# A two-layer hybrid block on one core: two small tiles take other places in SBUF

## The chip, the core and the metric

The kernel runs on one core of one Trainium2 chip. The metric is the time on the device in microseconds (us). Three timed runs of the kernel before gave 1068.19, 1068.74 and 1072.17 us; the median is 1068.74. A time is told below as ns where it belongs to one instruction.

## The reference, cut to what matters

Two layers work on a sequence of 256 tokens with 1024 features, in float32. Each layer is a mixer and a feed-forward part, both with a residual:

```
for l in range(2):
    h = rms_norm(x, norm_mix_w[l])
    q,k,v,qi,ki,wi,z,xbc,dt,g_attn,g_ssd = split(h @ w_in[l])
    a = attention over the 64 best keys by an index score      # 8 heads
    b = chunked state-space scan of silu(conv(xbc)), gated by silu(z), group norm
    x = x + (sigmoid(g_attn) * (a @ w_proj_attn) + sigmoid(g_ssd) * (b @ w_proj_ssd)) @ w_out
    h = rms_norm(x, norm_ffn_w[l])
    u = conv(h @ w_up) ; x = x + (silu(gate(u)) * val(u)) @ w_down
out = rms_norm(x, norm_final_w)
```

Nothing of this is touched by the change. By far the most work is the projections: 320 weight chunks of 128 rows are loaded, each is split into a high and a low part, and each is multiplied in three passes (high weights with the high and with the low part of the activations, low weights with the high part).

## The kernel before, in words

**How a projection runs.** Weights come by DMA from the SP queue into five `raw` buffers (L174). ScalarE casts a chunk to its high part `whi` (L199), VectorE subtracts to get `wlo` (L200). `n_outer` and `k_outer` then issue matmuls of 128 weight columns with 256 moving columns: `feed_high` (L376 with the high part of the activations, L377 with the low part), then `feed_low` (L382). In these the activations are the moving operand and the weights are loaded ahead. In the first projections of a layer (L548, L551, L554, function `wide`) it is the other way round: the weights move, in 308 or 512 columns, and the activations are loaded.

**Which tile holds what.** All activations and some weights lie in a pool `act`, where a tile is placed once by its tag, one after the other in the order of first use, and later tiles with the same tag take the same place. The tags that matter:

- `Bm`, `Cm`, `lg0`, `lg1`: the normed input of a layer or of the feed-forward part as `uh` (high) and `ul` (low), later the scan's B and C and the attention's logits.
- `big0`, `big1`: token-major projections, then `bc` (the scan's decay factors, read by the matmuls of L731), then `bL`, the low part of the scan's output. They also hold two early weight chunks (`ebig`).
- `s0` to `s3`: queries and keys, then `bH` (the high part of the scan's output), then `fH0`, `fL0`, `fH1`, `fL1` (the first third of the feed-forward's hidden values), and early weight chunks `es`.
- `hxh`, `hxl`: the scaled normed input (`hxh`, `hxl`) and the merged mixer output (`mH`, `mL`). `z0` to `z3` and `x0` to `x3` hold `aH`, `aL`, the scan's values, and `fH2` to `fH5` with their low parts.
- `wd` (320 bytes in a partition) holds the step sizes and index weights, `dec` (128 bytes) the decays of the scan's first chunk.

The weight buffers `whi`, `wlo` lie in a pool of their own ahead of `act`; all six start 64 bytes past a multiple of 256.

**What sets the order.** The engines' streams are written out by a scheduler at build time; helper work of attention and scan is laid between the projections as lanes of generators. A layer runs: input projections (to about 60 us in the first layer), convolution tiles with attention and scan between them (60 to 206), gates with z and the group norms (206 to 280), the scan's projection from `bH` and `bL` (280 to 325), the output projection from `mH`, `mL` (325 to 347), the feed-forward's first chunks from `uh`, `ul` (347 to 373), its other chunks from `hxh`, `hxl` (373 to 471), and the way down from `fH`, `fL` (471 to 531). The second layer repeats that about 525 us later. On the way down the first four output tiles run with the hidden values as the outer loop; the other four take, each in turn, 24 matmuls from `fH0`, `fL0`, `fH1`, `fL1`, then 24 from the next two pairs, then 18 from the last two. Each layer's group norms and norms put a matmul of `dg` with `ones` (L298, twice each) between the others.

Of the kernel before, what the change touches and what calls it, by code (L numbers as in the profile page):

```python
# [9 lines left out]
F32 = mybir.dt.float32  # L10
# [8 lines left out]
P = 128  # L19
# [44 lines left out]
def hybrid_kernel(ctx: ExitStack, tc: tile.TileContext, a: dict, out: bass.AP):  # L64
# [5 lines left out]
    act = ctx.enter_context(tc.tile_pool(name="act", bufs=1))  # L70
# [72 lines left out]
    def side(lane, gen, delay):  # L143


        lanes[lane].append([st["now"] + delay, gen])
# [100 lines left out]
    def sm(name, l=None, n=None):  # L247
        o, w = _SMALL[name]
        v = small[:, o:o + w]
        if l is not None:  # L250
            v = v[:, l * (w // L):(l + 1) * (w // L)]
        return v
# [150 lines left out]
        return ps  # L403


    nrm = Normed(sm("nmw", 0))
    side("norm", nrm.factor(), KD + 1)

    for l in range(L):

        tok = [act.tile([P, 8 * T], F32, name=f"big{t}", tag=f"big{t}")[:, :1856] for t in range(2)]
        V = [act.tile([P, T], F32, name=f"V{t}", tag=f"V{t}") for t in range(2)]
        wd = act.tile([P, 2, 40], F32, name="wd", tag="wd")

        def rotate(v, t, heads, dim, rot, o):
            h = rot // 2
# [83 lines left out]
        dA = act.tile([P, 2, 32], F32, name="dA", tag="dA")  # L500
        Pc = act.tile([P, 2, 32], F32, name="Pc", tag="Pc")
        nP = act.tile([P, 2, 32], F32, name="nP", tag="nP")
        dec = act.tile([P, 32], F32, name="dec", tag="dec")

        prd = dram.tile([32, 2, P], F32, name=f"prd{l}")

# [513 lines left out]
```

## Time and profile before

| what | value |
|---|---|
| median of the timed runs | 1068.74 us |
| time of the profiled execution | 1067.94 us |
| its span | 1066.1 us |
| mean granted TensorE clock, as a share | 0.999 |
| TensorE busy | 1056.1 us, 99% |
| VectorE busy | 860.7 us, 81% |
| ScalarE busy | 694.8 us, 65% |
| GpSimd busy | 81.4 us, 8% |
| mean DMA rate | 180 GB/s |

TensorE has work all the time, so the time is the sum of the paces at which its matmuls follow each other. A matmul's own duration in the profile (some 280 ns) spans several that are in flight, and is no measure of the pace; the pace is the distance between the starts of two neighbours, which the timeline shows, or a stretch divided by the matmuls that start in it.

### The profile page before, as it was taken

To read this page: it belongs to the slowest core of one execution; us is meant where nothing else is said; L and a number is where in the kernel's file an instruction comes from. 1 tells how busy PE (TensorE), PEld (TensorE's weight loads), DVE (VectorE), ACT (ScalarE), POOL (GpSimd) and SP (SyncE) were. 2 spreads that over 40 slices of the span, in tenths; PEclk is the share of its full clock that TensorE was granted. 3 is DMA by queue.
4 is the path that set the end of the run, shared out by engine and by line. 5 is a ranking of instruction groups with operands and counts; after the bars stand their busy time and mean duration, and the time that the engine had idled before them with its cause. 6 is when DMAs were issued, how large, how long until landed. Compare 5 with 4: busy or idle time off the path is not lost.

```text
span 1066.1 us, 22377 instructions
## 1 busy us (share of the span) xinstructions
PE 1056.1 (99%) x8713; PEld 1020.8 (96%) x8713; DVE 860.7 (81%) x1652; ACT 694.8 (65%) x1285; POOL 81.4 (8%) x88
## 2 busy tenths in 40 slices
PE   9999999999999999999999999999999999999997
PEld 8799999999999999999997999899999999999997
DVE  6999979789677898886577999887895878988643
ACT  6769878567555566665465789775674556666552
POOL 3000000033001000000100000000420020000011
PEclk9999999999999999999999999999999999999999
DMA  8655445555677256667645654554666761666661
GB/s 309 208 185 191 141 140 179 148 181 176 201 235 247 80 159 197 195 194 240 195 134 167 220 159 139 168 168 146 179 183 207 259 218 42 195 197 195 185 184 51
DMA packets 53688, 191.81 MB, mean 180 GB/s; under 512 B 6176, under 2 KB 7216, under 8 KB 52560
## 3 DMA queue, kind: packets, MB, share of 16 engines
q1 hardware_dynamic: 51840, 180.71, 54.5%
q0 software_dynamic: 1600, 9.69, 2.4%
q8 instruction: 68, 1.11, 0.4%
q14 instruction: 36, 0.29, 0.1%
q10 hardware_dynamic: 144, 0.01, 0.0%
HBM read 189.26 MB, written 1.11 MB: 179 GB/s over the span
## 4 chain that ended last, share of the span: by engine, by line
PE 87%; DMA 6%; DVE 3%; issue 1%; ACT 1%; POOL 0%; SPq 0%; POOLq 0%; DVEq 0%; ACTq 0%
PE acc L376 22%; PE acc L377 22%; PE acc L382 22%; DMA raw<-in_wu_dram 5%; PE acc L548 3%; PE acc L551 3%; PE acc L554 3%; PE sa L377 2%; PE sa L376 2%; PE sa L382 2%; PE sb L731 2%; DVE ul L330 1%; PE sa L615 1%; PE sa L640 1%; DVE wlo L200 1%
## 5 line engine op out<-in xcount | busy, mean ns | idle before, releaser
L199 ACT CAST whi<-raw 128x1024 fp32r<-128x1024 f32 (+2 forms) x320 | 332.0, 1040 | 225.2 <-PE acc L377 137.0
L200 DVE TENSOR_TENSOR wlo<-raw,whi 128x1024 fp32r<-128x1024 f32 (+2 forms) x320 | 386.5, 1210 | 102.1 <-ACT whi L199 95.4
L376 PE MATMUL acc<-hxh,whi 128*128 128x256 f32 x1456 | 352.3, 282 | 0.0
L377 PE MATMUL acc<-hxl,whi 128*128 128x256 f32 x1456 | 349.7, 280 | 0.0
L377 PEld LDWEIGHTS acc<-hxl,whi 128*128 128x128 f32 x1456 | 274.3, 188 | 1.8 <-issue 1.6
L376 PEld LDWEIGHTS acc<-hxh,whi 128*128 128x128 f32 x1456 | 274.3, 188 | 1.5 <-issue 1.2
L382 PE MATMUL acc<-hxh,wlo 128*128 128x256 f32 x1456 | 200.6, 279 | 0.0
L382 PEld LDWEIGHTS acc<-hxh,wlo 128*128 128x128 f32 x1456 | 182.0, 188 | 0.6 <-issue 0.5
L675 DVE SCALAR_TENSOR_TENSOR cv<-acc,half,cv 128x255 f32<-128x255 f32 (+2 forms) x144 | 66.6, 472 | 4.1 <-ACT cv L673 3.7
L877 DVE SCALAR_TENSOR_TENSOR cv<-acc,small,cv 128x255 f32<-128x255 f32 (+1 forms) x144 | 68.5, 477 | 1.3
L343 POOL TENSOR_TENSOR ssq<-ssq,sq 128x256 f32<-128x256 f32 x30 | 27.8, 928 | 498.4 <-ACT sq L339 495.1
L376 PE MATMUL acc<-fH,whi 128*128 128x256 f32 x264 | 64.0, 277 | 0.0
L377 PE MATMUL acc<-fL,whi 128*128 128x256 f32 x264 | 63.9, 277 | 0.0
L377 PEld LDWEIGHTS acc<-fL,whi 128*128 128x128 f32 x264 | 49.6, 188 | 0.0
L376 PEld LDWEIGHTS acc<-fH,whi 128*128 128x128 f32 x264 | 49.5, 188 | 0.0
L377 PE MATMUL acc<-bL,whi 128*128 128x256 f32 x192 | 47.6, 282 | 0.0
L376 PE MATMUL acc<-bH,whi 128*128 128x256 f32 x192 | 47.5, 279 | 0.0
L721 ACT ACTIVATE bc<-bc,nP 128x128 f32<-128x128 f32 x128 | 40.5, 392 | 7.5 <-DMA bc<-prd 7.4
L830 POOL TENSOR_TENSOR ssq<-ssq,sq 128x256 f32<-128x256 f32 x24 | 32.2, 1343 | 136.5 <-ACT sq L829 136.1
L875 ACT ACTIVATE cv<-acc,small 128x256 f32<-128x256 f32 x72 | 40.6, 563 | 0.1
L382 PE MATMUL acc<-fH,wlo 128*128 128x256 f32 x264 | 37.8, 277 | 0.0
L377 PEld LDWEIGHTS acc<-bL,whi 128*128 128x128 f32 x192 | 36.2, 188 | 0.0
(346 smaller groups left out, 2011.4 us busy)
## 6 DMA issues: line engine op xcount, KB each, us to landing
raw<-in_wu_dram SPq DMA_DIRECT2D x88, 512.0 KB, 4.0
raw<-in_wx_dram SPq DMA_DIRECT2D x48, 512.0 KB, 3.7
raw<-in_wd_dram SPq DMA_DIRECT2D x38, 512.0 KB, 3.7
raw<-in_wz_dram SPq DMA_DIRECT2D x32, 512.0 KB, 3.6
raw<-in_wp_dram SPq DMA_DIRECT2D x32, 512.0 KB, 4.4
raw<-in_wq_dram SPq DMA_DIRECT2D x24, 512.0 KB, 4.2
raw<-in_wgs_dram SPq DMA_DIRECT2D x16, 512.0 KB, 3.5
bc<-prd POOLq DMA_DIRECT2D x8, 1024.0 KB, 6.0
```

Of the source, the lines that this page charges most:

```text
L199: nc.scalar.copy(out=hi, in_=r)
L200: nc.vector.tensor_sub(lo, r, hi.bitcast(F32))
L376: nc.tensor.matmul(ps, wh[:, j, :], hi(k), start=first and j == 0, stop=False)
L377: nc.tensor.matmul(ps, wh[:, j, :], lo(k), start=False, stop=False)
L382: st["mm"] = nc.tensor.matmul(ps, wl[:, j, :], hi(k), start=False, stop=last and j == len(ks) - 1)
L548: nc.tensor.matmul(ps, hi[:, s], w[0], start=first, stop=False)
L551: nc.tensor.matmul(ps, lo[:, s], w[0], start=False, stop=False)
L675: nc.vector.scalar_tensor_tensor(v[:, j:], ps[:, :T - j], cw(l, 3 - j, i), v[:, j:], op0=OP.mult, op1=OP.add)
L721: nc.scalar.activation(E[:, h, :], E[:, h, :], AF.Relu, bias=nP[:, c, 8 * g + h:8 * g + h + 1])
L830: nc.gpsimd.tensor_add(acc, acc, sq)
L875: nc.scalar.activation(v, uu, AF.Identity, scale=fw(l, 2, i), bias=fb(l, i))
L877: nc.vector.scalar_tensor_tensor(v[:, j:], uu[:, :T - j], fw(l, 2 - j, i), v[:, j:], op0=OP.mult, op1=OP.add)
```

## The change

The tile `dec` is made once, ahead of the first norm, and no longer in each layer; the tile `wd` is made ahead of `big0` and no longer after `V`. No instruction is added or removed. The instructions stand in the same order on every engine, and wait for the same semaphores with the same counts.

```
+    dec = act.tile([P, 32], F32, name="dec")
     nrm = Normed(sm("nmw", 0))
     side("norm", nrm.factor(), KD + 1)
 
     for l in range(L):
 
+        wd = act.tile([P, 2, 40], F32, name="wd", tag="wd")
         tok = [act.tile([P, 8 * T], F32, name=f"big{t}", tag=f"big{t}")[:, :1856] for t in range(2)]
         V = [act.tile([P, T], F32, name=f"V{t}", tag=f"V{t}") for t in range(2)]
-        wd = act.tile([P, 2, 40], F32, name="wd", tag="wd")
...
         nP = act.tile([P, 2, 32], F32, name="nP", tag="nP")
-        dec = act.tile([P, 32], F32, name="dec", tag="dec")
```

What it does is to move addresses. The table gives where tiles start in a partition, as bytes past a multiple of 256, as the built programs have them:

| tiles | before | now |
|---|---|---|
| `whi`, `wlo`, `raw`, `xT` | 64 | 64 |
| `Bm`, `Cm`, `lg0`, `lg1` (`uh`, `ul`) | 64 | 192 |
| `big0`, `big1`, `V0`, `V1` (`bc`, `bL`, `ebig`) | 64 | 0 |
| `wd` | 64 | 192 |
| `s0` to `s3` (`bH`, `fH0`, `fL0`, `fH1`, `fL1`, `es`), `bias`, `dt`, `dA`, `Pc`, `nP` | 128 | 0 |
| `dec` | 128 | 64 |
| `hxh`, `hxl`, `ths`, `z0` to `z3`, `x0` to `x3`, all of the pool `tmp` | as before | as before |

Rows within these tiles are 512, 1024 or 2048 bytes apart, so the operands of L376, L377 and L382 have the same remainder as their tile.

## Rows read from the trace of the kernel before

**Rows 1.** The page: busy time of PE, and its granted clock in 40 slices.

```profile
PE 1056.1 (99%) x8713; PEld 1020.8 (96%) x8713; DVE 860.7 (81%) x1652; ACT 694.8 (65%) x1285; POOL 81.4 (8%) x88
...
PEclk9999999999999999999999999999999999999999
```

**Rows 2.** Stretches, PE alone (stretch, length, busy, count, clock, DMA): feed-forward, first layer.

```profile
372.70:470.63 97.93, 97.93 (x866) 1.00 0.61 185
470.63:481.94 11.31, 11.31 (x99) 1.00 0.65 182
481.94:500.98 19.04, 19.04 (x170) 1.00 0.73 235
...
503.81:508.58 4.77, 4.77 (x45) 1.00 0.65 225
```

**Rows 3.** Timeline of PE (start, length, what), way down, first layer.

```profile
502.87 1.10 PE L382 MATMUL acc<-fH,wlo 128*128 128x256 f32 x8
503.81 0.28 PE L376 MATMUL acc<-fH,whi 128*128 128x256 f32 x1
...
505.63 1.07 PE L382 MATMUL acc<-fH,wlo 128*128 128x256 f32 x8
506.54 0.28 PE L376 MATMUL acc<-fH,whi 128*128 128x256 f32 x1
```

**Rows 4.** Stretches, PE alone: other stages, in order of time.

```profile
60.00:206.00 146.00, 146.00 (x1237) 1.00 0.53 169
...
78.86:81.73 2.87, 2.87 (x26) 1.00 1.01 408
...
207.21:227.11 19.90, 19.90 (x171) 1.00 0.59 170
279.71:325.15 45.44, 45.44 (x387) 1.00 0.72 236
...
325.15:350.47 25.32, 25.32 (x218) 1.00 0.67 218
...
358.09:372.70 14.61, 14.61 (x127) 1.00 0.01 1
...
897.67:995.61 97.94, 97.94 (x866) 1.00 0.61 184
```

**Rows 5.** Timeline of PE around a scan matmul (L731), first layer.

```profile
205.19 0.28 PE L376 MATMUL acc<-aH,whi 128*128 128x256 f32 x1
...
205.98 0.28 PE L377 MATMUL acc<-aL,whi 128*128 128x256 f32 x1
206.19 1.09 PE L731 MATMUL sb<-bc,Xt 128*64 128x128 f32 x16
...
207.55 0.28 PE L376 MATMUL acc<-aH,whi 128*128 128x256 f32 x1
...
208.26 0.28 PE L382 MATMUL acc<-aH,wlo 128*128 128x256 f32 x1
```

**Rows 6.** Timeline of PE, chunks from the early tiles, second layer after a norm's matmuls.

```profile
879.53 0.63 PE L382 MATMUL acc<-uh,es 128*128 128x256 f32 x4
880.00 0.63 PE L382 MATMUL sa<-uh,es 128*128 128x256 f32 x4
```

**Rows 7.** The same place in the first layer.

```profile
354.67 0.62 PE L382 MATMUL acc<-uh,es 128*128 128x256 f32 x4
355.12 0.62 PE L382 MATMUL sa<-uh,es 128*128 128x256 f32 x4
```

**Rows 8.** Timeline of PE, input projections of the second layer, weights moving.

```profile
547.84 0.62 PE L551 MATMUL acc<-whi,ul 128*128 128x512 f32 x2
548.29 0.62 PE L554 MATMUL acc<-wlo,uh 128*128 128x512 f32 x2
```

**Rows 9.** Groups by line and shape, DVE: the same subtraction into tiles at different addresses.

```profile
L200 DVE TENSOR_TENSOR wlo<-raw,whi 128x1024 fp32r<-128x1024 f32 x308 | 375.7, 1222 | 97.7 <-ACT whi L199 92.9 <-PE acc L554 2.2 <-PE acc L382 0.3
...
L200 DVE TENSOR_TENSOR es<-raw,es 128x1024 fp32r<-128x1024 f32 x4 | 4.9, 1226 | 6.0 <-ACT es L199 5.9
```

More of the change, by code (lines that the diff above doesn't have):

```diff
@@ L403, in n_outer @@
         return ps
+    dec = act.tile([P, 32], F32, name="dec")
     nrm = Normed(sm("nmw", 0))
@@ L409, in hybrid_kernel @@
     for l in range(L):
+        wd = act.tile([P, 2, 40], F32, name="wd", tag="wd")
         tok = [act.tile([P, 8 * T], F32, name=f"big{t}", tag=f"big{t}")[:, :1856] for t in range(2)]
         V = [act.tile([P, T], F32, name=f"V{t}", tag=f"V{t}") for t in range(2)]
-        wd = act.tile([P, 2, 40], F32, name="wd", tag="wd")
         def rotate(v, t, heads, dim, rot, o):
@@ L502, in hybrid_kernel @@
         nP = act.tile([P, 2, 32], F32, name="nP", tag="nP")
-        dec = act.tile([P, 32], F32, name="dec", tag="dec")
         prd = dram.tile([32, 2, P], F32, name=f"prd{l}")
```

## The prediction

> **What bounds the kernel now.** I read the page first: TensorE is busy 99% of the span, VectorE 81%, ScalarE 65%, and the granted clock is full in all slices [rows 1], which is the higher of the two levels, 2.4 GHz. So the time is the sum of the paces of TensorE's matmuls, and a change helps or hurts only through these paces, or if it starves TensorE. Second I cut the trace into stretches by stage. The counts in rows 2 and 4 take in two or three matmuls that were in flight when the stretch opened; I divide by the matmuls that the program issues in it. The first stretch, the other chunks of the feed-forward, is 97.93 us for 864 matmuls, 113.3 ns each. The next, the way down from the tiles `fH0`, `fL0`, `fH1`, `fL1`, is 11.31 us for 96 of the same shape: 117.8 ns. The next, from `fH2` and on, is 19.04 us for 168: 113.3 ns again [rows 2]. Third, the timeline shows that this follows the tile and not the hour: on the way down the pace changes within a few matmuls, each time the moving operand changes its tile. Eight low-weight matmuls from `fH0` and `fH1` take 0.94 us from the first start to the start behind them, 117.5 ns each; the next eight of the same kind, from `fH2` and `fH3`, take 0.91, 113.8 ns [rows 3]. Nothing differs between the two but the operand's address: `fH0` starts 128 bytes past a multiple of 256, `fH2` at one, the weights 64 past one.
>
> So there are two paces, fast (113.3 ns) and slow (117.8 ns), 4.45 ns apart. I call the moving operand's address minus the weights' address, modulo 256, the difference. At 64 all long stretches but short beginnings are slow (`fH0`, and 124 matmuls in 14.61 us from `uh` [rows 4]). At 192 both occur: fast in the feed-forward of both layers (97.94 us for 864 in the second), slow in the gates (19.90 us for 168) and in the output projection and what follows (25.32 us for 215 distances) [rows 2, 4]. Where `bH` (64) and `bL` (0) take turns it is worst: 45.44 us for 384, 118.3 ns [rows 4]. At 0 alone, two early chunks, 2.87 us for 24, 119.6 ns [rows 4].
>
> At 192 the pace has a memory. It stays through hundreds of matmuls and is thrown over, to either side, by float32 matmuls between: before the scan's matmuls at 206.19 seven distances take 0.79 us (113 ns), behind them six take 0.71 (118 ns), and so it stays for the 20 us that follow [rows 4, 5]. After the same norm matmuls the second layer goes on slowly (0.47 us for four) and the first fast (0.45) [rows 6, 7].
>
> **The change part by part.** It adds and removes no instruction and no wait. The difference becomes 192 for all of L376, L377 and L382 but 48 matmuls of two early chunks. 1,440 of 7,392 come there from another one: 384 on the way down from `fH0` to `fL1` (from 64), 288 from `uh`, `ul` with early chunks (from 64), 768 from `bH`, `bL` (from 64 and 0).
>
> - Way down. The stretch is entered from `hxh` at the fast pace and nothing is laid between, so it should go on at 113.3 as `fH2` does. 192 in each layer x 4.45 ns = 0.85 us, two layers: -1.7 us.
> - `uh`, `ul`. If they end in the fast pace, as the first layer's beginning shows [rows 7], 124 in each layer x 4.45 = 0.55, two layers: -1.1 us. If slow: 0.
> - `bH`, `bL`. They are entered from the gates, which are slow now. At the slow pace the turns go (118.3 to 117.8): 384 x 0.5 = 0.2, two layers: -0.4 us. At the fast pace it would be 384 x 5.0 = 1.9 in each.
> - Input projections, where the weights move. Their difference goes from 0 to 128 (in the early chunks to 64), which no row shows. Now two of 512 columns take 0.45 us, 226 ns each [rows 8], which is the fast pace for twice the columns. From below nothing is to be had; from above the slow pace, 235.6 ns, for 288 matmuls: +2.7 us. The 192 of 308 columns can move by 5 ns each to either side, about 1 us. I take 0, the nearest row, and keep -1 to +3.7.
> - 60 to 206 us and its repetition [rows 4]. The main operands keep their difference, but the scan's and attention's matmuls between them (`bc`, `V`, `kk4` and the logits move) may throw the pace over elsewhere. 865 matmuls of a layer lie there, and a bit over half of them are fast in the timeline; all slow or all fast would be +2 or -2 us in a layer. I take 0.
> - VectorE and ScalarE. The subtraction of L200 takes 1222 ns into tiles 64 past a multiple and 1226 into `es`, 128 past [rows 9]. No cost; and TensorE is the one that is waited for.
>
> Sum: -1.7 - 1.1 - 0.4 = -3.2 us on the profiled execution's 1067.94 (span 1066.1 and 1.8 around it): 1064.7. The median of the runs is 0.8 above that execution, so 1065.5.
>
> The Trainium skill speaks against all this: "SBUF — State Buffer", section "SBUF: two separate sides", says that TensorE never waits on anyone at its port, and its section "Operand start alignment" treats a start address as a matter of legality alone, with nothing timed. By that rule the sum would be 0. Rows 2 and 3 disagree: the same instruction is 4% slower from one address than from another.
>
> **The rivals.**
>
> 1. *The feed-forward falls into the slow pace.* Now the 64 of `uh` stands between the mixer and the feed-forward, and behind it the 864 matmuls are fast in both layers [rows 2, 4]. With 192 everywhere the pace is handed on: output projection (slow now), norm matmuls, `uh`, the two matmuls of `dg`, and then with nothing between to the layer's end. If the last of these leaves it slow, 864 and 336 matmuls cost 4.45 ns more, 5.3 us in a layer, and the gains on the way down and at `uh` are lost. Against it: the same norm matmuls left one layer fast [rows 7]. For it: they left the other slow [rows 6]. It decides where `dg` ends, at about 358 us and 883 us. One layer: -0.85 - 0.55 - 0.4 + 5.3 = +3.5, 1072.2. Both: +10.6 - 0.4 = +10.2, 1079.0, slower than before.
> 2. *The middle becomes fast too.* If the scan's matmuls at 206 leave the fast pace now that `bc` starts 64 bytes lower, some 590 matmuls to 280 us gain 2.6 us, `bH` and `bL` a further 1.7, and the 216 behind them 0.96: 5.2 in a layer. One layer 1060.3, both 1055.1. For it: before that place the pace is fast [rows 5]. Against it: norm matmuls follow that leave it slow as often as not.
> 3. *The address is not what decides.* Then nothing moves: 1068.7. Against it stands the way down, where only the tile differs [rows 3].
>
> **How the numbers follow.** Forecast (fast feed-forward, slow middle) 0.42, rival 1 0.25 (half one layer, half both), rival 2 0.22, rival 3 0.11. The forecast's own range, by the input projections and the 60 to 206 us, is 1061.5 to 1070. A measurement tells 0.5% (5.3 us) from no change: faster is below 1063.4, slower above 1074.1. Faster: rival 2 and a quarter of the forecast, 0.33. Slower: the half of rival 1 with both layers, and a little of the rest, 0.17. Within: 0.50. The range runs from both layers of rival 2 to near both layers of rival 1: 1055 to 1078.
>
> **What would show it right or wrong.** In the changed kernel's trace the stretch of 96 matmuls behind the 864 should be 10.9 us and not 11.3; the 864 themselves should be 97.9 in both layers (rival 1: 101.8); `bH`, `bL` 45.2 for 384 (rival 2: 43.5); the gates after the last scan matmul 19.9 for 168 (rival 2: 19.0). Wrong altogether if stretches at difference 192 show paces other than these two, or if VectorE or a DMA is waited for where it was not.

## The result and the profile after

The changed kernel takes 1078.76 us (median of 4 runs, 1078.05 to 1080.57) against 1069.41 for the kernel before, run beside it: a ratio of 1.0086, interval 1.0062 to 1.011. It is slower, by 9.4 us at the medians. The forecast was 1065.5; the first rival, with both layers, had been worked out at 1079.0.

The page of the profiled execution (1078.41 us): TensorE is still busy 99% of a span that has grown by 10.5 us, and the clock is full but for the last slice [rows 1].

```profile
span 1076.6 us, 22377 instructions
...
PE 1065.9 (99%) x8713; PEld 1029.2 (96%) x8713; DVE 861.5 (80%) x1652; ACT 696.8 (65%) x1285; POOL 81.4 (8%) x88
...
PEclk9999999999999999999999999999999999999998
```

So the loss is in the paces of matmuls. Stretches of the changed kernel, PE alone (stretch, length, busy, count with what was in flight, clock, DMA share, GB/s): `uh` behind `dg`, the 864 of `hxh`, the 96 from `fH0` to `fL1`, the 168 from `fH2` on, the second layer's `hxh`, the gates behind the scan, `bH` and `bL`.

```profile
358.57:372.65 14.08, 14.08 (x127) 1.00 0.00 1
372.65:474.40 101.75, 101.75 (x866) 1.00 0.60 179
474.40:485.71 11.31, 11.31 (x98) 1.00 0.64 179
485.71:505.50 19.79, 19.79 (x171) 1.00 0.75 230
902.87:1004.63 101.76, 101.76 (x866) 1.00 0.59 177
208.41:228.30 19.89, 19.89 (x170) 1.00 0.57 173
281.03:326.28 45.25, 45.25 (x387) 1.00 0.72 237
```

The 124 matmuls of `uh` went from 14.61 to 14.08 us, 113.5 ns each, and the same 14.08 us in the second layer: the gain is there. The 864 behind them went from 97.93 and 97.94 to 101.75 and 101.76, 117.8 ns each, and the 168 from 19.04 to 19.79 [rows 2, 4]. Gates, `bH` and `bL` are as forecast in the first layer. So the slow pace begins between `uh` and `hxh`. The timeline of PE there (start, length, what) shows the place:

```profile
358.45 0.28 PE L298 MATMUL sb<-dg,ones 128*128 128x256 f32 x1
358.57 0.64 PE L382 MATMUL sa<-uh,ez 128*128 128x256 f32 x4
359.04 0.28 PE L376 MATMUL acc<-uh,ez 128*128 128x256 f32 x1
```

```profile
372.19 0.62 PE L382 MATMUL acc<-uh,epT 128*128 128x256 f32 x4
372.65 0.28 PE L376 MATMUL acc<-hxh,whi 128*128 128x256 f32 x1
372.76 0.28 PE L377 MATMUL acc<-hxl,whi 128*128 128x256 f32 x1
372.88 0.28 PE L376 MATMUL acc<-hxh,whi 128*128 128x256 f32 x1
373.00 0.28 PE L377 MATMUL acc<-hxl,whi 128*128 128x256 f32 x1
```

Four matmuls behind `dg` take 0.47 us to the next start, 117.5 ns each, but then `uh` settles at 113.3. The last four from `uh` take 0.46 us, and from the first `hxh` on it is 0.35 for three and 117.8 on the mean. Nothing lies between. What jumps there are both addresses at once: the moving operand from 192 past a multiple of 256 to 0, the weights from 0 (`epT`) to 64 (`whi`). Their difference stays 192.

### The profile page after: what moved, and what is told of

The parts are those of the page before. It is cut to its first block, busy times and chain, and to the rows that moved or that the text cites. A ratio compares the mean times of both kernels' runs of the same rounds, so it can differ in the third digit from the quotient of the medians.

```text
span 1076.6 us, 22377 instructions
## 1 busy us (share of the span) xinstructions
PE 1065.9 (99%) x8713; PEld 1029.2 (96%) x8713; DVE 861.5 (80%) x1652; ACT 696.8 (65%) x1285; POOL 81.4 (8%) x88
## 4 chain that ended last, share of the span: by engine, by line
PE 88%; DMA 6%; DVE 3%; issue 1%; ACT 1%; POOL 0%; POOLq 0%; SPq 0%; DVEq 0%; ACTq 0%
PE acc L376 22%; PE acc L377 22%; PE acc L382 22%; DMA raw<-in_wu_dram 5%; PE acc L548 3%; PE acc L551 3%; PE acc L554 3%; PE sa L377 2%; PE sa L376 2%; PE sa L382 2%; PE sb L731 2%; DVE ul L330 1%; PE sa L615 1%; PE sa L640 1%; DVE wlo L200 1%
## 5 line engine op out<-in xcount | busy, mean ns | idle before, releaser
L376 PE MATMUL acc<-hxh,whi 128*128 128x256 f32 x1456 | 357.3, 284 | 0.0
L377 PE MATMUL acc<-hxl,whi 128*128 128x256 f32 x1456 | 354.7, 282 | 0.0
L377 PEld LDWEIGHTS acc<-hxl,whi 128*128 128x128 f32 x1456 | 275.2, 189 | 1.8 <-issue 1.6
L376 PEld LDWEIGHTS acc<-hxh,whi 128*128 128x128 f32 x1456 | 275.0, 189 | 1.5 <-issue 1.2
L382 PE MATMUL acc<-hxh,wlo 128*128 128x256 f32 x1456 | 203.3, 281 | 0.0
L382 PEld LDWEIGHTS acc<-hxh,wlo 128*128 128x128 f32 x1456 | 184.4, 189 | 0.6 <-issue 0.5
L377 PE MATMUL acc<-fL,whi 128*128 128x256 f32 x264 | 65.3, 281 | 0.0
L376 PE MATMUL acc<-fH,whi 128*128 128x256 f32 x264 | 65.3, 281 | 0.0
L377 PEld LDWEIGHTS acc<-fL,whi 128*128 128x128 f32 x264 | 49.9, 189 | 0.0
L376 PEld LDWEIGHTS acc<-fH,whi 128*128 128x128 f32 x264 | 49.9, 189 | 0.0
L376 PE MATMUL acc<-bH,whi 128*128 128x256 f32 x192 | 47.2, 281 | 0.0
L377 PE MATMUL acc<-bL,whi 128*128 128x256 f32 x192 | 47.1, 280 | 0.0
L382 PE MATMUL acc<-fH,wlo 128*128 128x256 f32 x264 | 38.6, 281 | 0.0
L376 PEld LDWEIGHTS acc<-bH,whi 128*128 128x128 f32 x192 | 36.3, 189 | 0.1
```

The costliest lines, as they stand in the source:

```text
L376: nc.tensor.matmul(ps, wh[:, j, :], hi(k), start=first and j == 0, stop=False)
L377: nc.tensor.matmul(ps, wh[:, j, :], lo(k), start=False, stop=False)
L382: st["mm"] = nc.tensor.matmul(ps, wl[:, j, :], hi(k), start=False, stop=last and j == len(ks) - 1)
```

## The experiments

Theory 1: TensorE's pace in these matmuls depends on the difference of the two addresses and on a phase that is handed on; the loss is the phase in which `hxh` begins. "Phase" is my name for whatever makes a stretch fast or slow at the same difference; no view shows it, only the pace that comes of it. The rivals are that the moved tiles are slow by themselves (A, B), that other engines make it (C, E), and that the absolute address counts (D).

**Each half of the change alone, and a third placement (e1_dec, e2_wd, e3_s0).**

```
# e1_dec                                    # e2_wd                         # e3_s0
+    dec = act.tile([P, 32], ...)           +  wd = ...  (ahead of tok)        wd = ...
     nrm = Normed(sm("nmw", 0))                tok = ...; V = ...           +  dec = act.tile(...)
...                                         -  wd = ...                     ...
-        dec = act.tile([P, 32], ...)                                          qiT = ...   # tag s0
                                                                            ...
                                                                            -  dec = ...
```

> The kernel before with only the decays' tile moved ahead of the first stage's input (uh and ul start 192 past a multiple of 256, big0, big1, V and wd 192, the tiles s0 to s3 at 0). Theory 1 (the pace of TensorE follows the difference of moving and weight address, and the slow pace of the feed-forward is set where uh ends and hxh begins): uh is at 192 and the feed-forward at 192 as in the changed kernel, so it falls into the slow pace in both layers: 1078.5 us, 1077 to 1080. Rival A (the move of the big tiles to 0 is what costs): about 1068 to 1069. If only one layer falls: 1073.

Measured: 1079.02, ratio 1.0086 (1.0062 to 1.0109). The stretches of `uh` and `hxh`:

```profile
360.81:374.89 14.08, 14.08 (x127) 1.00 0.01 1
374.89:476.64 101.75, 101.75 (x866) 1.00 0.60 179
```

> The kernel before with only the step sizes' tile moved ahead of the big tiles (big0, big1 and V start 128 past a multiple of 256; uh, ul stay at 64, s0 to s3 at 128). Theory 1: uh stays at difference 64, so the feed-forward is entered as before, at the fast pace: 1068 to 1069.5. Rival A (the big tiles): 1075 to 1079.

Measured: 1068.88, ratio 1.0006 (0.9987 to 1.0025). The same two stretches:

```profile
358.61:373.22 14.61, 14.61 (x127) 1.00 0.01 1
373.22:471.15 97.93, 97.93 (x866) 1.00 0.61 184
```

The move of `dec` alone makes the whole loss, and the big tiles moved alone (to 128) cost nothing. That weakens rival A but does not end it: in e1_dec `big0`, `big1` and `V` have moved too, to 192, beside `uh`, `ul` and `s0` to `s3`.

> The kernel before with the decays' tile placed between wd and s0: uh, ul and the big tiles stay at 64, the tiles s0 to s3 go to 0, which is difference 192 on the way down and for bH. Theory 1: the feed-forward is entered from difference 64 and so at the fast pace, the way down goes on fast: the gain of 0.85 us a layer without the loss, 1067 to 1068.5 (feed-forward 97.9 us for 864, way down 10.9 for 96). Rival B (tiles s0 to s3 at 0 are what makes the feed-forward slow, as wherever they moved it went slow): 1077 or more.

Measured: 1078.44, ratio 1.0073 (1.0048 to 1.0099), and this is a miss for theory 1 as I had put it. The two stretches in the first and the second layer:

```profile
358.92:372.98 14.06, 14.06 (x127) 1.00 0.01 1
372.98:474.74 101.76, 101.76 (x867) 1.00 0.60 180
888.31:902.91 14.60, 14.60 (x126) 1.00 0.00 1
902.91:1004.67 101.76, 101.76 (x866) 1.00 0.59 177
```

`uh` is at difference 64, and in the first layer it ran at 113.4 ns there, in the second at 117.7; behind both, `hxh` is slow. So "entered from 64" does not make `hxh` fast. More than the difference is handed on, or rival B is right. Nor is the outcome the same in every run: the nine runs lie between 1069.53 and 1081.68 us, where the four of the changed kernel lie within 2.5 us. Only one of the nine has a trace.

**The paces on an otherwise idle core (m1_paces).** 57 stretches of 24 matmuls for each weight address, so that each difference follows each other one.

```
for wo in (0, 64):                 # weights 128, then 192 past a multiple of 256
    for s in circuit():            # 0, 32, ... 224, each entered from each
        run(24, wo, 32 * s)        # moving address = weight address + 32 s
```

> A kernel that computes none of the reference: 160 matmuls to warm up, then stretches of 24 float32r matmuls of 128x256, each stretch at another difference of moving and weight address (0, 32, ... 224, every one entered from every other), the whole once with the weights 128 past a multiple of 256 and once 192 past; nothing else runs. Theory 1: 117.8 ns at 64, 120 at 0, and at 192 either 113.3 or 117.8 by what came before, the same in both halves. Rival C (the paces come from contention with what the other engines read and write): one pace, 113.3 ns, at all differences. Rival D (the absolute address decides): the two halves differ, in the second half each pace stands 64 bytes further.

Stretches of that kernel, PE alone: difference 64; 0; 192 behind 0; 192 behind 128; 192 behind 64; and in the second half 192 behind 128.

```profile
57.49:60.31 2.82, 2.82 (x26) 1.00 0.00 0
68.81:71.69 2.88, 2.88 (x27) 1.00 0.00 0
71.69:74.43 2.74, 2.74 (x27) 1.00 0.00 0
82.84:85.67 2.83, 2.83 (x26) 1.00 0.00 0
94.21:96.93 2.72, 2.72 (x26) 1.00 0.02 6
...
244.44:247.27 2.83, 2.83 (x26) 1.00 0.02 6
```

With no other engine at work the paces are there: 2.82 us for 24 at 64 (117.5 ns), 2.88 at 0 (120), and at 192 either 2.72 to 2.75 (settled at 113.3 to 113.6) or 2.83 (117.9). From the starts of the matmuls: 192 came out fast behind 0, 32, 64 and 160, and slow behind 96, 128 and 224; 32, 96, 128, 160 and 224 lie between 116.5 and 120.2 on the mean. The two halves agree stretch by stretch within 0.13 ns in all 56. Rival C has fallen, since no other engine is at work, and so has D as far as a shift of 64 bytes tests it: the absolute address did not make the pace. The Trainium skill says on "TensorE: Matmul & The Clock Gate", section "Step-by-step: what each phase is for", that loading the next weights takes no read bandwidth in SBUF from the running matmul. These stretches speak against it for this kind of matmul: with everything else idle, where the weights lie relative to the moving operand costs up to 6%. How the two reads get in each other's way is not seen in a trace and stays open.

**What throws the pace over (m2_flips).**

```
chunk(0, base); chunk(0, 192)              # base 96 or 32
one(wh, mh, k, 0, d)   # 1, 2 or 4 times   # or, in place of this line and the next:
chunk(0, 192)                              # chunk(s, 192), both addresses s further
...
```

> A kernel that computes none of the reference and looks for what throws the pace over: chunks of 24 float32r matmuls in the order of the feed-forward (a weight block twice, for high and low part, then eight low weights), always 24 at difference 192 that were entered from difference 96 (slow there so far) or from 32 (fast there so far), then one, two or four matmuls at another difference (0, 16, ... 240), or both addresses moved together by 32 to 224 bytes, then 24 at 192 again. Theory 1, as it now stands (192 has a fast and a slow phase, handed on until something of another spacing shifts it): single matmuls flip the phase in some of the cases, the same ones whenever repeated, and a joint shift of both addresses by 64 flips fast to slow, as at the changed kernel's start of hxh. Rival E (only other engines or a stall flip it): all the second stretches keep the pace of the first.

Stretches of that kernel, two and two: at 192, then both addresses 64 further; at 192, one matmul at difference 80 (not in the rows), at 192 again; at 192, one matmul at 64, at 192 again.

```profile
744.93:747.67 2.74, 2.74 (x26) 1.00 0.00 0
747.67:750.50 2.83, 2.83 (x27) 1.00 0.00 0
161.44:164.26 2.82, 2.82 (x26) 1.00 0.00 0
164.38:167.11 2.73, 2.73 (x26) 1.00 0.00 0
549.47:552.20 2.73, 2.73 (x26) 1.00 0.00 0
552.32:555.15 2.83, 2.83 (x27) 1.00 0.00 0
```

A joint step of 64, with the difference unchanged, turned fast to slow (2.74 to 2.83 us), both times it was tried: that is the step from `uh`, `epT` to `hxh`, `whi` in the changed kernel. So did joint steps of 32, 128, 192 and 224; steps of 96 and 160 left it fast, each the same way twice. One matmul at difference 80 left the fast pace behind it, from slow (2.82 to 2.73) and from fast; one at 64 turned fast to slow. All 31 cases that came twice from the same pace (24 with added matmuls, 7 joint steps) came out the same both times. What fell is the label "from 96 slow, from 32 fast": of 52 stretches behind 96, 33 were fast, and of 37 behind 32, 29. What is handed on has more values than the two paces show. That is how the miss above can be read: two stretches at the same pace need not hand on the same. Rival E has fallen: nothing but matmuls ran in these stretches, and none of them waited.

**One matmul more, in the kernel (k1, k2, k3).** The cause can now be tried where it matters: ahead of the second chunk from `hxh`, with the operand read 144 or 128 bytes in; the chunk's own first matmul overwrites its result.

```
+            if kick is not None and i == 0:
+                nc.tensor.matmul(ps, wh[:, 0, :], kick, start=True, stop=True)
...
+            self.kick = h.rearrange("p k t -> p (k t)")[:, 36:292]     # 32:288 for difference 64
...
-            pv = n_outer([(hi, lo, range(8))])
+            pv = n_outer([(hi, lo, range(8))], nrm.kick if i == 4 else None)
```

> The changed kernel with one matmul more in each layer, ahead of the second chunk from hxh: same weights, moving operand the tile hxh read 144 bytes in, so at difference 80; its result is overwritten by the chunk itself. On the idle chip one such matmul left the fast pace behind it from either side. Theory 1 (the loss is the slow phase handed on at the start of hxh): about 840 matmuls of the feed-forward and 336 of the way down gain 4.45 ns, 5.2 us a layer, less two matmuls of 0.12: 1078.8 - 10.2 = 1068.6, 1067 to 1070; 864 distances of hxh in 98.1 us. Rival A (tiles at these addresses are slow by themselves, or because other engines write beside them): 1079.

Measured: 1068.91, ratio 0.9996 (0.9982 to 1.0011); the 10 us are back. Stretches: first chunk from `hxh`, the other 840, the 96 from `fH0` on, the 168 from `fH2`, the second layer's 840.

```profile
372.59:375.42 2.83, 2.83 (x27) 1.00 0.00 0
375.54:470.74 95.20, 95.20 (x842) 1.00 0.62 189
470.74:481.62 10.88, 10.88 (x98) 1.00 0.61 188
481.62:500.66 19.04, 19.04 (x170) 1.00 0.71 236
899.89:995.10 95.21, 95.21 (x843) 1.00 0.63 189
```

The first chunk is slow (118 ns); behind one matmul of 0.12 us (start 375.42) everything to the layer's end is at 113.3, the way down from `fH0` too: 10.88 us for 96, the gain that was forecast. Rival A has fallen: every tile lies where the change put it.

> As the one before, but the added matmul reads 128 bytes in, difference 64, which on the idle chip left the slow pace behind it. Theory 1: the feed-forward stays slow, 1078.8 + 0.25 = 1079. Rival F (any matmul put in there, or the stall it makes, would bring the fast pace): 1069.

Measured: 1079.34, ratio 1.0096 (1.0075 to 1.0117). Rival F has fallen: the same instruction from an address 16 bytes lower leaves the 840 slow.

```profile
375.57:474.50 98.93, 98.93 (x843) 1.00 0.61 185
```

> The kernel before, no tile moved, with the one matmul at difference 64 in each layer ahead of the second chunk from hxh. Theory 1: the fast pace that it had there turns slow for about 840 matmuls, and for the first tiles of the way down nothing changes (they are slow at 64 anyway); fH2 and on come from 64 again and are fast. 840 x 4.45 = 3.7 us a layer, 7.5 in all, and 0.25 for the matmuls: 1068.5 + 7.7 = 1076.2, 1074.5 to 1078. Rival A: 1068.7.

Measured: 1078.97, ratio 1.0095 (1.0075 to 1.0114), 2.8 us above the value expected. First chunk, the other 840, the 168 from `fH2`:

```profile
372.63:375.36 2.73, 2.73 (x26) 1.00 0.00 0
375.48:474.41 98.93, 98.93 (x843) 1.00 0.62 185
...
485.72:505.50 19.78, 19.78 (x170) 1.00 0.75 240
```

The kernel before, no tile moved, loses the same 10 us by one matmul in each layer. The direction is theory 1's. The size was off since `fH2` stayed slow (19.78, not 19.04): the 96 at difference 64 in between, 117.8 ns before and now, hand the phase on instead of resetting it.

**Can the rest be had (k4, x1, x2, x3)?** Four such matmuls in each layer (the first z chunk, the pair n = 6, the first of `bH`, `bL`, and the one above):

> The changed kernel with four matmuls at difference 80 in each layer: ahead of the first z chunk behind the scan, of the third last pair of chunks of the mixer (n = 6), of the first pair of bH, bL, and of the second chunk from hxh as before. Theory 1: besides the 10.2 us of the feed-forward, about 130 matmuls behind the scan (0.6 us), some 45 ahead of bH, the 384 of bH, bL and the 192 behind them (2.6 us) become fast in each layer: 1068.6 - 6.4 + 0.7 = 1063, 1061 to 1066, faster than both. If only the feed-forward answers: 1069.5. Rival A: 1079.5.

Measured: 1069.51, ratio 0.9997 (0.9981 to 1.0014); its profiled execution took 1064.66. That is a miss: two of the twelve runs lie in the 1061 to 1066 that was expected. In the trace seven of the eight added matmuls have a fast stretch behind them; so the 152 matmuls behind the scan take 17.24 us in the first layer (113.4 ns). In the second layer scan matmuls still follow the first one, and the stretch behind them is slow. And inside `bH`, `bL` TensorE now runs into a late weight chunk, and behind it the pace is slow again (stretch, then timeline):

```profile
210.52:227.76 17.24, 17.24 (x155) 1.00 0.59 168
```

```profile
310.58 0.39 PE L378 MATMUL acc<-bH,whi 128*128 128x256 f32 x1 [0.21 <-ACT whi L200]
```

Last, the third placement with the reset, to ask rival B:

> The kernel before with the decays' tile between wd and s0 (tiles s0 to s3 at 0, uh and ul at 64, as in the run where the feed-forward came out slow), and one matmul at difference 80 ahead of the second chunk from hxh in each layer. Theory 1 (a phase is handed on, and such a matmul leaves the fast one whatever came before): the feed-forward and the whole way down are fast; against the profiled run with the tiles s0 to s3 at 0 (1078.4) 2 x 5.2 us less: 1068, and 1064 to 1067 without the stretch at lower clock that this run had at 353 us. Rival B (s0 to s3 at 0 make it slow): 1078.

Measured: 1068.85, ratio 0.9997 (0.9981 to 1.0013). First chunk of the first layer; then, of the second layer, first chunk and the other 840:

```profile
374.71:377.44 2.73, 2.73 (x26) 1.00 0.00 0
...
899.73:902.56 2.83, 2.83 (x27) 1.00 0.02 6
902.68:997.89 95.21, 95.21 (x843) 1.00 0.63 189
```

Rival B has fallen: the same tiles at the same places, and 840 matmuls at 113.3. But only the second layer tests the added matmul. In the first the chunk ahead of it is fast already (2.73 us), with every tile placed as in e3_s0, where that chunk was slow. The two programs are the same up to there, so with these tiles the phase at the start of `hxh` is not the same in every run.

Laid side by side, the twelve traces of whole kernels show what that start hangs on. Of the 24 steps from `uh` to `hxh`, 13 come from a fast `uh` (its last 24 matmuls; ten layers at 192, three at 64), and behind all 13 `hxh` is slow; 11 come from a slow `uh` at 64, and behind ten of them `hxh` is fast. The one that is not is the second layer of e3_s0.

The run x1_s0_plus80 is also a good place to see a gain go. From the starts of neighbouring matmuls its paces add up to 4.6 us less than those of the kernel before (`bH` to `mL` 3.3, way down 1.7, 0.4 lost elsewhere), yet its span is 1067.5 against 1066.1. Waits of PE at the feed-forward's norm in both layers (waiting for, us in total, times, longest), and the 35 matmuls behind each:

```profile
PE sb L362 <- POOL ssq L343: 1.2, 1, 1.2
```

```profile
353.89:359.62 5.73, 5.73 (x37) 0.70 0.36 111
879.47:885.20 5.73, 5.73 (x38) 0.70 0.36 114
```

TensorE arrives earlier and waits for GpSimd's sum of squares, 1.2 us in each layer where it was 0.7 and 0.4; and behind the wait the granted clock is 0.70, partly at the lower level, so that 35 matmuls take 5.73 us. The kernel before needed 4.05 and 4.20 at full clock. So the lower clock costs 3.2 us there, the longer waits 1.4, and a late weight chunk at 311 us 0.6 (two distances of 620 and 222 ns): 5.2 of the 6.0 that went.

> As the one before, with a second such matmul in each layer, ahead of the first z chunk behind the scan. Theory 1: about 150 matmuls behind the scan become fast as well, 0.66 us a layer less 0.12: 1 us below the run before. If time that TensorE saves there comes back as a wait for weights: no difference.

Measured: 1068.1, ratio 0.9993 (0.9976 to 1.0009): nothing that can be told apart.

> As the first of these, with the added matmul ahead of every eighth chunk from hxh (five in each layer). If the scatter between runs (1066 to 1072 with one such matmul) comes from the pace falling back within the feed-forward, the runs lie closer together and the median is 1 to 2 us lower; if it comes from elsewhere, the median is 0.9 us higher, for eight matmuls of 0.12.

Measured: 1070.03, ratio 0.9996 (0.9981 to 1.0012); 1065.8 to 1072.3, no closer than the 1066.1 to 1072.2 with one reset. That speaks against chunks from `hxh` falling back as what spreads the runs; what does stays open. In its own trace all chunks from `hxh` were fast in both layers, the one ahead of the first added matmul too, and the pace fell back once, half way down in the first layer. No version here beats the kernel before.

## Why the prediction was wrong

Excess over 113.3 ns of each matmul's distance to the next, summed by stage, both layers, us:

| term | forecast | measured |
|---|---|---|
| way down, `fH0` to `fL1` | -1.7 | 0.0 |
| `uh`, `ul` | -1.1 | -1.4 (the 124 of each layer: -1.1) |
| `bH`, `bL` | -0.4 | -0.9 |
| input projections | 0 (-1 to +3.7) | +1.4 |
| 60 to 206 us | 0 | +0.2 |
| the 864 from `hxh` | 0 | +7.6 |
| way down from `fH2` on | 0 | +2.9 |
| output projection from `mH`, second layer | 0 | -0.8 |

That is 9.0 us, without the stalls. At the norms of the feed-forward TensorE waited 1.5 us for GpSimd against 1.0, and ahead of two weight chunks of the second layer (841.6 and 876.3 us) it lost 0.7 us against 0: 10.2 of the 10.5 us of the span.

- What bounds the kernel was right: no engine's work changed, TensorE's paces made all of it, and both paces are the two that were read from the trace. Rival 3, the address doesn't matter, is refuted by k1 and k2, whose only difference is 16 bytes in one operand.
- The step that failed is in the part on the way down: "The stretch is entered from `hxh` at the fast pace". It carried over the fast feed-forward of before [rows 2, 4] without asking what made it fast, and it took a pace to pass on unchanged where the difference does not change. Neither held. In the kernel before a slow `uh` at 64 goes over into a fast `hxh`; the change made `uh` fast at 192, and both addresses step by 64 behind it. In all ten such layers here `hxh` came out slow: 101.75 us for 864 where 97.9 was forecast.
- Rival 1 had the outcome and the price (4.45 ns for 1,200 matmuls, 5.3 us a layer; 10.5 us measured for both), but its deciding place was wrong: behind `dg` the pace is fast in both layers. It is decided at 372.65 us, where both addresses step by 64. The second kernel on the idle core shows that this step alone turns fast to slow. That `dg` should decide came from rows 6 and 7, where the two layers differ, and made the rival look like a coin toss at 0.25; the range stopped at 1078, short of the rival's own 1079.0. The step to `hxh` was the same in both layers and was not looked at, since the difference does not change there. That its 1079.0 comes so near 1078.76 is in part luck: it counted `uh` as lost (-1.4 measured), and had no term for the input projections' +1.4, the output projection's -0.8 or the 1.2 us of longer stalls.
- `uh` at 113.3, gates and `bH` at 117.8 came as forecast. In the second layer TensorE lost 0.2 us at 841.6 us, ahead of a weight chunk, and `bH` and most of the output projection went on at the fast pace; the forecast had no term for that. At 876.3 us it waited 0.3 us for VectorE, where it had not before: one of the forecast's own signs of being wrong, true in small.
- The input projections stayed inside their bounds, at +1.4: the median distance between 512-column matmuls went from 227 to 232 ns. The forecast had read 226 off one pair of rows 8, as the fast pace with nothing to gain below it; a quarter of these distances were 231 ns or more already.

Left open: which event sets the phase at other places (two layers still differ in places), and why the clock falls behind some waits and not behind others. A wait of 1.3 us at the same place in the changed kernel's second layer is followed by full clock, one of 1.0 us in the second layer of x2_s0_two by 0.70. Open is also why the start of `hxh` differs between e3_s0 and x1_s0_plus80, with all tiles at the same places.

## What to carry to other kernels

When tiles move in SBUF and nothing else does, compare the paces of equal matmuls stretch by stretch, and look for the first matmul at the new pace: the cause stands there, and one added or shifted matmul ahead of it tells cause from company. Where a pace is a state that is handed on, ask of each fast stretch what put it there before you count on it. And a stage that is sped up ahead of a wait can give its time to the wait, and, as in x1_s0_plus80, more than that to the clock behind it.

## What the runs showed of the hardware

- Float32r matmuls of 128x256 with a weight load each, nothing else running: 113.3 ns at best, and of the differences that are multiples of 32 only at 192; 117.8 at 64, 120 at 0, and 117.8 at 192 as well, by the phase in which the stretch is entered (m1_paces). In a kernel 64 had a fast phase too: 14.06 us for 124 in e3_s0.
- The phase is kept through hundreds of matmuls (1,368 in k1) and is changed by a single matmul from another address or by a step of both addresses. On the idle core the same step from the same pace had the same outcome each time (31 cases, twice each); in the kernel not always: from a slow `uh` at 64 ten steps out of eleven led to a fast `hxh`.
- A shift of all addresses by 64 bytes made no difference: 56 stretches repeated there agreed within 0.13 ns.
- Behind waits of 1.2 us at the feed-forward's norm the granted clock was 0.70 over the next 35 matmuls, which took 5.73 us (x1_s0_plus80); behind a wait of 1.3 us in the changed kernel it was full, and 35 took 4.06.
